# An encoder layer on one core: low weight tiles at another offset, two more first transposes, token block 0 finished first, and longer runs of high and low products in the up projection

## The chip, the core and the metric

The kernel runs on one of the eight cores of a Trainium2 chip. A core has a matmul engine (PE, with its weight loads shown as PEld), a vector engine (DVE), an activation engine (ACT), a general engine (POOL), a queue engine that issues most transfers (SP), and sixteen DMA engines between its on-chip memory and HBM. The metric is the device time of one execution in microseconds; the median of three runs is given.

## The reference

One layer of an encoder on 256 tokens of width 2048, and a final normalisation:

```
h = rms_norm(x);  proj = h @ w_in                    # 2048 x 9216
y_a = gated spatial MLP of (u, v)                    # 8 groups, chunks of 128 tokens
y_b = neighbourhood attention of (q, k, v)           # 16 heads on a 4 x 64 grid
merged = sigmoid(g_a) * (y_a @ Wb_a) + sigmoid(g_b) * (y_b @ Wb_b)
x = x + merged @ w_out
h = rms_norm(x);  up = h @ w_up                      # 2048 x 11008
up = depthwise conv of width 3 over tokens
x = x + (silu(gate) * val) @ w_down                  # 5504 x 2048
return rms_norm(x)
```

All inputs and outputs are float32, and the weights, some 64 million numbers, are read once.

## The kernel before, in words

**Products.** Each float32 operand is split in two: a high part, rounded by ACT to the matmul's own 32-bit format (`high`, L267), and a low part, the rest, which DVE subtracts (`low`, L270). A product is then three matmuls: high by high, low token part by high weight, and high token part by low weight.

**The stream of weights.** The weights are laid out in the order of use, in pieces of at most 128 x 1024 numbers (512 KB), and `weight_stream` names the order: the first group, the u and v columns, the attention's q, k and v with the gates between them, the branches, the output projection, and then twice an up projection over half of the 43 channel tiles and the down projection that follows it. For each piece i, `begin` issues loads as far as raw buffers are free (five), converts pieces up to i + 4 (`prepare`, as far as a pair of high and low buffers is free: four, and two more from the output projection on), and runs the tasks that earlier steps have put down for it (copies out of the banks, the convolution, and so on). Then the group's step writes the matmuls of piece i. Nothing else sets the order: each engine runs its instructions in the order in which the program was written, and waits on tiles. `unit_done` gives a pair of buffers back, and a later piece's conversion waits until the matmuls that read them are over.

**Weight-stationary groups.** The u columns, q and k, and the up projection (kind `ws`) hold the weights in the array and stream the tokens through. The token tile has the high parts of the 256 tokens and then their low parts, so one matmul of 512 columns on a high weight tile (L371) makes two of the three products, and one of 256 columns on a low weight tile (L377) the third. A piece has two row tiles by four column tiles of 128, so eight high products and eight low ones; a group has eight pieces and four banks. `spread_products` writes the high ones first in even pieces and the low ones first in odd pieces, so that across pieces they stand in runs of 16. Of the up projection there are 21 such groups, and one with two banks.

**The low tile's place.** A low tile is allocated with 64 numbers to spare (`LINE`), and in `ws` groups its data begin at `LOW_AT` numbers. All weight tiles and token tiles of the program begin 224 bytes past a multiple of 256; low data of `ws` groups therefore lie on a multiple of 256 before.

**The end.** The last group, the down projection's second half of columns, keeps its last four pieces back and finishes one bank after the other (`by_block`), each with 12 matmuls: the two token blocks t of 128 tokens by two column blocks of 512. As a bank is done, `finish` adds it to the residual on DVE, squares it on ACT with a sum, and multiplies by the final norm's weights (third quarter on POOL, fourth on DVE). `root` makes one over the root of the mean square for a token block, and `scaled` multiplies a stretch of columns by it on DVE or ACT and issues its store.

**The start.** `keep_awake` puts `WAKE` transposes of an identity ahead of the first product (L599), which start as soon as the identity is made.

Of the kernel before, what the change touches and what calls it, by code (L numbers as in the profile page):

```python
# [8 lines left out]
F32 = mybir.dt.float32  # L9
F32R = mybir.dt.float32r  # L10
AF = mybir.ActivationFunctionType
OP = mybir.AluOpType
AX = mybir.AxisListType
PSUM = bass.MemoryType.PSUM

T = 256
D = 2048
# [19 lines left out]
RMS_EPS = 1e-6  # L37
# [2 lines left out]
BLOCK = 1024  # L40
AHEAD = 5
RAW, UNITS, HALVES = 5, (4, 2), 1
WAKE = 18
EARLY = 4
SPLIT = 3
LINE = 64
LOW_AT = 8

FF_BLOCKS = ((0, 22), (22, 43))
FF_SEVEN = ((3, 5, 7), (2, 4, 6))  # L50
# [106 lines left out]
def trunk_kernel(ctx, tc, x, weights, vectors, ln_g, ln_b, w_s_turned, b_s, rpb, norm_final, out):  # L157
    nc = tc.nc
# [14 lines left out]
    const = keep("const")  # L173
    wpool = keep("weights")
    tmp = keep("tmp")
    hpool = keep("hT")
# [19 lines left out]
    pieces, _ = weight_pieces()  # L196
    kinds = {key: g[0] for key, g in weight_stream()[0].items()}
    size_of = {key: len(g[2]) for key, g in weight_stream()[0].items()}
    starts = {}
# [51 lines left out]
    def unit_done(key):  # L251
        slot = units.pop(key)[2]
        if slot[0] not in gone:
            unit_free.append(slot)
# [106 lines left out]
        prepare(i + AHEAD - 1)  # L361
        run_tasks(i)

    def spread_products(ps, n, last, i, acts, m):
        h, l, _ = units[i]
        tiles = len(pieces[i][2])

        def highs(k):
            for b, p in enumerate(ps):
                c = k * m + b * 128  # L370
                nc.tensor.matmul(p, h[:, c:c + 128], acts(2 * n + k), start=n == 0 and k == 0,  # L371
                                 stop=last and k == tiles - 1)

        def lows(k):
            for b, p in enumerate(ps):
                c = k * m + b * 128
                nc.tensor.matmul(p[:, :T], l[:, c:c + 128], acts(2 * n + k)[:, 0, :], start=False, stop=False)  # L377

        for f in (highs, lows) if n % 2 == 0 else (lows, highs):
            for k in range(tiles):  # L380
                f(k)

    def three_products(p, x, w, start, stop):
        xh, xl = x
# [47 lines left out]
    def ws_step(key, acts, done):  # L432
        box = {}

        def step(i):
            n, last = i - starts[key], i == starts[key] + size_of[key] - 1
            m = pieces[i][5]
            if n == 0:
                box["ps"] = [bank() for _ in range(m // 128)]
            spread_products(box["ps"], n, last, i, acts, m)  # L440
            unit_done(i)
            if last:
                done(box["ps"], i + 1)
        return step

    def wide_step(key, acts, sevens, rest, done, by_block=0, fresh=None):
# [70 lines left out]
        def step(i):  # L517
            n = i - n0
            c0, c1 = slice(0, 512), slice(512, 1024)
            if n in firsts:  # L520
                k = tiles[n]
                h, l, _ = halves[i]
                hb, lb, _ = units[i, "b"]
                product(1, acts(k, 0), (h, l))
                product(2, acts(k + 1, 0), (hb[:, c0], lb[:, c0]))
                product(3, sevens(k)[3], (hb[:, c1], lb[:, c1]))
                half_free.append(halves.pop(i)[2])
                unit_done((i, "b"))
            elif n - 1 in firsts:
                k = tiles[n - 1]  # L530
                ht, lt, _ = units[i - 1, "t"]
                hs, ls, _ = units[i - 1, "s"]
                S = sevens(k)
                product(5, S[0], (ht[:, c0], lt[:, c0]))
                product(7, S[2], (ht[:, c1], lt[:, c1]))
                unit_done((i - 1, "t"))
                product(6, S[1], (hs[:, c1], ls[:, c1]))
                product(4, acts(k + 1, 1), (hs[:, c0], ls[:, c0]))
                unit_done((i - 1, "s"))
                if n - 1 == firsts[-1]:  # L540
                    combine(i)
            elif n < size - by_block:
                h, l, _ = units[i]
                for (b, c), u in OUT.items():
                    cs = slice(c * 512, (c + 1) * 512)
                    product(u, acts(tiles[n], b), (h[:, cs], l[:, cs]))
                unit_done(i)
            elif n == size - 1:
                for b, c in ((0, 0), (1, 0), (0, 1), (1, 1)):
                    u = OUT[b, c]  # L550
                    for m in range(size - by_block, size):
                        h, l, _ = units[n0 + m]
                        cs = slice(c * 512, (c + 1) * 512)
                        product(u, acts(tiles[m], b), (h[:, cs], l[:, cs]))
                    done(p(u), b, c, i + 1)
                    free(p(u))
                for m in range(size - by_block, size):
                    unit_done(n0 + m)
            if n == size - 1 and not by_block:
                for (b, c), u in OUT.items():  # L560
                    done(p(u), b, c, i + 1)
                    free(p(u))
# [601 lines left out]
    def finish(p, t, q):  # L1164
        x2, ss = rs["x2"], fin["ss"]
        if q == 2:
            add_down(p, t, 2)
            v = x2[:, t, 1024:1536]
            nc.gpsimd.tensor_mul(v, v, fin["g", 2])
            part = fin["part", t] = const.tile([128, 1], F32, name=f"part{t}")  # L1170
            nc.vector.tensor_reduce(part, ss[:, t, 0:3], axis=AX.X, op=OP.add)
            nc.vector.tensor_scalar(part, part, 1.0 / D, RMS_EPS, op0=OP.mult, op1=OP.add)
            return
        v = x2[:, t, 1536:]
        nc.vector.tensor_add(v, p, v)
        nc.scalar.activation(junk, v, AF.Square, accum_out=ss[:, t, 3:4])
        fin["y", t] = hpool.tile([128, 512], F32, name=f"h{t}")
        if t == 0:
            nc.vector.tensor_mul(fin["y", 0], v, fin["g", 3])
            root(0)  # L1180
        else:
            scaled(0, 0, 512, nc.vector, nc.sync)
            scaled(0, 512, 1024, nc.vector, nc.sync)
            root(1, lambda: (nc.vector.tensor_mul(fin["y", 1], v, fin["g", 3]),
                             scaled(0, 1024, 1536, nc.scalar, nc.sync)))
            scaled(1, 640, 1536, nc.scalar, nc.scalar)
            scaled(1, 0, 640, nc.vector, nc.sync)
            scaled(1, 1536, 2048, nc.vector, nc.sync)
            scaled(0, 1536, 2048, nc.vector, nc.sync)

    def root(t, meanwhile=None):
        a, r, q, e, both = (const.tile([128, 1], F32, name=f"{n}3{t}") for n in "arqeb")
        nc.vector.tensor_scalar(a, fin["ss"][:, t, 3:4], 1.0 / D, fin["part", t], op0=OP.mult, op1=OP.add)
        nc.scalar.activation(q, a, AF.Sqrt)
        if meanwhile:
            meanwhile()
        nc.vector.reciprocal(r, q)
        nc.vector.scalar_tensor_tensor(e, r, r, a, op0=OP.mult, op1=OP.mult)
        nc.vector.tensor_scalar(e, e, -0.5, 1.5, op0=OP.mult, op1=OP.add)
        nc.vector.tensor_mul(both, r, e)  # L1200
        fin["r", t] = both
# [205 lines left out]
```

## Time and profile before

| what | value |
| --- | --- |
| median of three runs | 1315.31 us (1315.12 to 1316.0) |
| profiled execution, own time | 1315.79 us |
| its span, first to last instruction | 1313.6 us |
| granted matmul clock, mean | 0.998 |
| PE, PEld, DVE, ACT, POOL busy | 1302.2, 1109.9, 1015.1, 746.9, 99.5 us |
| high products in `ws` groups (L371) | 1760, 426.4 us busy |
| low products in `ws` groups (L377) | 1760, 228.5 us busy |
| up projection, two stretches | about 596 to 843 us and 959 to 1193 us |
| sum that follows the last matmul | starts at 1303.97 us |

How to read the rows: a group gives line, engine, operation, output tile, operands and shape, the count, busy microseconds and the mean nanoseconds of one, and idle time before it with what ended it. A row of the timeline gives start, length, engine, line, operation, tiles, shape and count. Matmuls are pipelined, so the length of one is longer than its share of the time; the distance from one start to the next is what it costs. A row of the chain of waits gives start, length, what ran, and how many in a row. A row of waits gives who waited for whom, the sum, how often, and the longest.

### The profile page before, as it was taken

The page shows a single profiled execution, that of the slowest core. Times are in us where ns is not written, and L with a number is a line of the kernel's source. Part 1 is how long each engine was busy: PE and PEld are TensorE (multiplying, and loading weights), DVE is VectorE, ACT ScalarE, POOL GpSimd, SP SyncE. Part 2 cuts the span into 40 slices and gives each one's busy share as a digit, 9 for nine tenths or more (in the row PEclk, how much of TensorE's full clock was granted, in tenths as well). Part 3 has the DMA queues.
Part 4 walks back from the last instruction along what each step waited for, and adds up shares of the span by engine and source line. Part 5 has one row for each costly group of instructions (what it writes and reads, how often), then busy time and mean ns, then how long its engine had stood idle before and what let it go on. Part 6 is the DMA issues. An engine that isn't in the chain of part 4 may idle for free.

```text
span 1313.6 us, 18614 instructions
## 1 busy us (share of the span) xinstructions
PE 1302.2 (99%) x6752; PEld 1109.9 (84%) x6752; DVE 1015.1 (77%) x1485; ACT 746.9 (57%) x1103; POOL 99.5 (8%) x192
## 2 busy tenths in 40 slices
PE   9999999999999999999999999999999999999997
PEld 8888888888888888888888888888888888888885
DVE  5577667767588978887878787898958787869987
ACT  5755567576545545555655555554535555546554
POOL 0502065430000000000000000000000000000000
PEclk9999999999999999999999999999999999999999
DMA  8957685655646566665655656557656656546653
GB/s 329 320 177 208 206 223 183 202 160 177 192 158 243 181 202 233 220 207 176 193 193 186 197 181 203 165 172 234 210 186 192 192 191 194 180 142 224 230 171 128
DMA packets 74044, 261.42 MB, mean 199 GB/s; under 512 B 9568, under 2 KB 10720, under 8 KB 73440
## 3 DMA queue, kind: packets, MB, share of 16 engines
q1 hardware_dynamic: 69984, 252.46, 59.3%
q0 software_dynamic: 3680, 7.30, 2.1%
q8 instruction: 53, 0.87, 0.3%
q10 hardware_dynamic: 288, 0.47, 0.1%
q14 instruction: 39, 0.32, 0.1%
HBM read 256.00 MB, written 2.10 MB: 196 GB/s over the span
## 4 chain that ended last, share of the span: by engine, by line
PE 92%; DMA 3%; DVE 3%; ACT 1%; issue 1%; POOL 0%; DVEq 0%; ACTq 0%; POOLq 0%
PE bank L371 29%; PE bank L377 15%; PE bank L386 15%; PE bank L388 15%; PE bank L387 15%; DMA wraw<-in_weights_dram 2%; DMA start<-in_weights_dram 1%; DVE wlo L270 1%; ACT whi L267 1%; PE bank L868 1%; PE bank L920 0%; PE bank L599 0%; PE bank L404 0%; PE bank L403 0%; DVE x L1034 0%
## 5 line engine op out<-in xcount | busy, mean ns | idle before, releaser
L270 DVE TENSOR_TENSOR wlo<-wraw,whi 128x1024 fp32r<-128x1024 f32 (+1 forms) x476 | 571.0, 1216 | 158.6 <-ACT whi L267 154.4
L267 ACT ACTIVATE whi<-wraw 128x1024 fp32r<-128x1024 f32 (+1 forms) x476 | 489.0, 1046 | 240.8 <-PE bank L387 76.3
L371 PE MATMUL bank<-h,whi 128*128 128x512 f32 x1760 | 426.4, 393 | 0.0
L371 PEld LDWEIGHTS bank<-h,whi 128*128 128x128 f32 x1760 | 321.6, 188 | 64.2
L377 PEld LDWEIGHTS bank<-h,wlo 128*128 128x128 f32 x1760 | 224.5, 188 | 10.3 <-DVE wlo L270 0.5
L377 PE MATMUL bank<-h,wlo 128*128 128x256 f32 x1760 | 228.5, 281 | 0.3 <-DVE wlo L270 0.3
L386 PE MATMUL bank<-whi,h 128*128 128x512 f32 x284 | 111.8, 394 | 0.0
L388 PE MATMUL bank<-wlo,h 128*128 128x512 f32 x284 | 110.7, 390 | 0.0
L387 PE MATMUL bank<-whi,h 128*128 128x512 f32 x284 | 110.6, 389 | 0.0
L388 PE MATMUL bank<-wlo,a 128*128 128x512 f32 x248 | 96.6, 389 | 0.0
L386 PE MATMUL bank<-whi,a 128*128 128x512 f32 x248 | 96.5, 389 | 0.0
L387 PE MATMUL bank<-whi,a 128*128 128x512 f32 x248 | 96.5, 389 | 0.0
L1097 ACT ACTIVATE tc<-ta,vec 128x256 f32<-128x256 f32 x86 | 47.1, 594 | 84.3 <-DVE ta L1095 84.3
L734 DVE TENSOR_TENSOR ta<-bank,tb 128x256 f32<-128x256 f32 x110 | 39.0, 417 | 67.2 <-ACT tb L732 67.2
L732 ACT ACTIVATE tb<-bank 128x256 f32<-128x256 f32 x110 | 36.2, 383 | 90.7 <-PE bank L371 85.1
L388 PEld LDWEIGHTS bank<-wlo,h 128*128 128x128 f32 x284 | 53.3, 188 | 11.3
L386 PEld LDWEIGHTS bank<-whi,h 128*128 128x128 f32 x284 | 53.3, 188 | 11.0
L387 PEld LDWEIGHTS bank<-whi,h 128*128 128x128 f32 x284 | 53.4, 188 | 10.7
L388 PEld LDWEIGHTS bank<-wlo,a 128*128 128x128 f32 x248 | 46.5, 188 | 10.0 <-DVE wlo L270 0.3
L387 PEld LDWEIGHTS bank<-whi,a 128*128 128x128 f32 x248 | 46.6, 188 | 9.7
L386 PEld LDWEIGHTS bank<-whi,a 128*128 128x128 f32 x248 | 46.5, 188 | 9.6
L1354 POOL DMA_DIRECT2D h<-in_norm_final_dram x4 | 2.2, 540 | 674.7 <-DVE wlo L270 674.2
(209 smaller groups left out, 1584.0 us busy)
## 6 DMA issues: line engine op xcount, KB each, us to landing
wraw<-in_weights_dram SPq DMA_DIRECT2D x446, 512.0 KB, 4.4
start<-in_weights_dram SPq DMA_DIRECT2D x13, 640.0 KB, 6.0
xs<-in_x_dram SPq DMA_DIRECT2D x2, 1024.0 KB, 10.1
vw<-va POOLq DMA_DIRECT2D x32, 64.0 KB, 5.9
x<-in_x_dram POOLq DMA_DIRECT2D x2, 1024.0 KB, 9.1
wraw<-in_weights_dram SPq DMA_DIRECT2D x8, 256.0 KB, 2.8
run<-in_rpb_dram POOLq DMA_DIRECT2D x64, 31.2 KB, 4.3
out_dram<-x SPq DMA_DIRECT2D x5, 256.0 KB, 2.9
```

The lines of the kernel that those rows point to most:

```text
L267: nc.scalar.activation(h, w, AF.Copy)
L270: nc.vector.tensor_sub(l, w, h.bitcast(F32))
L371: nc.tensor.matmul(p, h[:, c:c + 128], acts(2 * n + k), start=n == 0 and k == 0, stop=last and k == tiles - 1)
L377: nc.tensor.matmul(p[:, :T], l[:, c:c + 128], acts(2 * n + k)[:, 0, :], start=False, stop=False)
L386: nc.tensor.matmul(p, xh, wh, start=start, stop=False)
L387: nc.tensor.matmul(p, xl, wh, start=False, stop=False)
L388: nc.tensor.matmul(p, xh, wl, start=False, stop=stop)
L732: nc.scalar.activation(t, p[:, T:], AF.Copy)
L734: nc.vector.tensor_add(a, p[:, :T], t)
L868: nc.tensor.matmul(o, Q[s][:, c], k.rearrange("p (r c) -> p r c", r=ROWS)[:, :, k0:k0 + UNION], start=n == 0, stop=n == 1)
L1097: nc.scalar.activation(v, u, AF.Identity, scale=ck[:, 1, ch:ch + 1], bias=ck[:, 3, ch:ch + 1])
L1354: nc.gpsimd.dma_start(fin["g", j], bass.AP(tensor=norm_final.tensor, offset=norm_final.offset + j * 512, ap=[[0, 128], [1, 512]]))
```

## The change

Four edits:

1. `LOW_AT` goes from 8 to 56 numbers, so the low data of `ws` groups begin 224 bytes into their tile instead of 32.
2. `WAKE` goes from 18 to 20.
3. `spread_products` gets the group's first piece, its size and a flag. With the flag (the up projection alone) pieces are taken in fours: the highs of piece 0 and piece 1, the lows of 0, 1, 2 and 3, the highs of 2 and 3; so low products, and high ones across groups of four, stand in runs of 32. Buffers are given back in pairs, behind the odd piece. Without the flag the order is as before.
4. At the end, the banks are finished in the order (t 0, third quarter), (t 0, fourth), (t 1, third), (t 1, fourth), where the third quarters of both blocks came first. `finish` is written for it: block 0's root follows its fourth quarter, its first 1024 columns are scaled by ACT and stored at once, its third quarter by DVE behind block 1's third sum, and its fourth quarter behind block 1's fourth sum.

```diff
-WAKE = 18
+WAKE = 20
...
-LOW_AT = 8
+LOW_AT = 56
...
-    def spread_products(ps, n, last, i, acts, m):
-        h, l, _ = units[i]
-        tiles = len(pieces[i][2])
-
-        def highs(k):
...
-        for f in (highs, lows) if n % 2 == 0 else (lows, highs):
+    def spread_products(ps, first, n, size, acts, m, long):
+
+        last = size - 1
+
+        def highs(n):
+            h = units[first + n][0]
+            tiles = len(pieces[first + n][2])
             for k in range(tiles):
-                f(k)
+                for b, p in enumerate(ps):
+                    c = k * m + b * 128
+                    nc.tensor.matmul(p, h[:, c:c + 128], acts(2 * n + k), start=n == 0 and k == 0,
+                                     stop=n == last and k == tiles - 1)
+
+        def lows(n):
+            l = units[first + n][1]
+            for k in range(len(pieces[first + n][2])):
+                for b, p in enumerate(ps):
+                    c = k * m + b * 128
+                    nc.tensor.matmul(p[:, :T], l[:, c:c + 128], acts(2 * n + k)[:, 0, :], start=False, stop=False)
+
+        fours = (((highs, n),), ((highs, n), (lows, n - 1), (lows, n)), ((lows, n),),
+                 ((lows, n), (highs, n - 1), (highs, n)))
+        twos = ((highs, n), (lows, n)), ((lows, n), (highs, n))
+        for f, k in fours[n % 4] if long else twos[n % 2]:
+            f(k)
+        if not long:
+            unit_done(first + n)
+        elif n % 2:
+            unit_done(first + n - 1)
+            unit_done(first + n)
...
-            spread_products(box["ps"], n, last, i, acts, m)
-            unit_done(i)
+            spread_products(box["ps"], starts[key], n, size_of[key], acts, m, key[0] == "up")
...
-                for b, c in ((0, 0), (1, 0), (0, 1), (1, 1)):
-                    u = OUT[b, c]
+                for (b, c), u in OUT.items():
...
-            part = fin["part", t] = const.tile([128, 1], F32, name=f"part{t}")
-            nc.vector.tensor_reduce(part, ss[:, t, 0:3], axis=AX.X, op=OP.add)
-            nc.vector.tensor_scalar(part, part, 1.0 / D, RMS_EPS, op0=OP.mult, op1=OP.add)
+            if t == 0:
+                first_squares(0)
+            else:
+                scaled(0, 1024, 1536, nc.vector, nc.sync)
             return
...
-        fin["y", t] = hpool.tile([128, 512], F32, name=f"h{t}")
+        if t == 1:
+            first_squares(1)
+            scaled(0, 1536, 2048, nc.vector, nc.sync)
+        y = fin["y", t] = hpool.tile([128, 512], F32, name=f"h{t}")
+        nc.vector.tensor_mul(y, v, fin["g", 3])
+        root(t)
         if t == 0:
-            nc.vector.tensor_mul(fin["y", 0], v, fin["g", 3])
-            root(0)
+            scaled(0, 0, 1024, nc.scalar, nc.sync)
         else:
-            scaled(0, 0, 512, nc.vector, nc.sync)
-            scaled(0, 512, 1024, nc.vector, nc.sync)
-            root(1, lambda: (nc.vector.tensor_mul(fin["y", 1], v, fin["g", 3]),
-                             scaled(0, 1024, 1536, nc.scalar, nc.sync)))
             scaled(1, 640, 1536, nc.scalar, nc.scalar)
             scaled(1, 0, 640, nc.vector, nc.sync)
             scaled(1, 1536, 2048, nc.vector, nc.sync)
-            scaled(0, 1536, 2048, nc.vector, nc.sync)
```

`first_squares` is the pair of steps taken out of `finish` (the sum over three quarters, and the mean with its epsilon), and `root` loses the work that was put under its square root.

Inside an up group, at its fifth piece, the matmul engine changes from high products to low ones here (`whi` and `wlo` are weight tiles, `h` a token tile):

```order
L371 MATMUL bank3_6032<-h9_5825,whi4_6028 128x512
L371 MATMUL bank1_6033<-h9_5825,whi4_6028 128x512
L371 MATMUL bank2_6034<-h9_5825,whi4_6028 128x512
L371 MATMUL bank7_6035<-h9_5825,whi4_6028 128x512
L377 MATMUL bank3_6032<-h8_5824,wlo4_6029 128x256
L377 MATMUL bank1_6033<-h8_5824,wlo4_6029 128x256
L377 MATMUL bank2_6034<-h8_5824,wlo4_6029 128x256
L377 MATMUL bank7_6035<-h8_5824,wlo4_6029 128x256
```

and in the changed kernel at the same place (high products are written at its line 374, low ones at its line 382):

```order
L374 MATMUL bank3_6034<-h9_5827,whi4_6030 128x512
L374 MATMUL bank1_6035<-h9_5827,whi4_6030 128x512
L374 MATMUL bank2_6036<-h9_5827,whi4_6030 128x512
L374 MATMUL bank7_6037<-h9_5827,whi4_6030 128x512
L374 MATMUL bank3_6034<-h10_5837,whi5_6048 128x512
L374 MATMUL bank1_6035<-h10_5837,whi5_6048 128x512
L374 MATMUL bank2_6036<-h10_5837,whi5_6048 128x512
L374 MATMUL bank7_6037<-h10_5837,whi5_6048 128x512
```

The next piece's high products have come ahead of this piece's low ones.

Behind the last matmul, from the sum of the last bank on, DVE has before:

```order
L1175 TENSOR_TENSOR x2_5085<-bank4_12066,x2_5085 128x512
L1209 TENSOR_SCALAR x2_5085<-x2_5085,b30_12444 128x512 x2
L1193 TENSOR_SCALAR a31_12470<-ss_3_162,part1_12421 128x1
L1184 TENSOR_TENSOR h1_12465<-x2_5085,h5_11746 128x512
L1197 RECIPROCAL r31_12471<-q31_12472 128x1
L1198 SCALAR_TENSOR_TENSOR e31_12473<-r31_12471,a31_12470 128x1
L1199 TENSOR_SCALAR e31_12473<-e31_12473 128x1
L1200 TENSOR_TENSOR b31_12474<-r31_12471,e31_12473 128x1
L1209 TENSOR_SCALAR x2_5085<-x2_5085,b31_12474 128x640
L1209 TENSOR_SCALAR x2_5085<-h1_12465,b31_12474 128x512
L1209 TENSOR_SCALAR x2_5085<-h0_12438,b30_12444 128x512
```

and in the changed kernel (a, q, r, e and b are the steps of `root`, numbered 30 for block 0 and 31 for block 1):

```order
L1186 TENSOR_TENSOR x2_5087<-bank4_12068,x2_5087 128x512
L1203 TENSOR_REDUCE part1_12468<-ss_3_164 128x1
L1204 TENSOR_SCALAR part1_12468<-part1_12468 128x1
L1222 TENSOR_SCALAR x2_5087<-h0_12422,b30_12428 128x512
L1192 TENSOR_TENSOR h1_12473<-x2_5087,h5_11748 128x512
L1208 TENSOR_SCALAR a31_12475<-ss_3_164,part1_12468 128x1
L1210 RECIPROCAL r31_12476<-q31_12477 128x1
L1211 SCALAR_TENSOR_TENSOR e31_12478<-r31_12476,a31_12475 128x1
L1212 TENSOR_SCALAR e31_12478<-e31_12478 128x1
L1213 TENSOR_TENSOR b31_12479<-r31_12476,e31_12478 128x1
L1222 TENSOR_SCALAR x2_5087<-x2_5087,b31_12479 128x640
L1222 TENSOR_SCALAR x2_5087<-h1_12473,b31_12479 128x512
```

Two scalings of block 0 have left this place and one has moved up, the two small steps of `first_squares` have come in, and the multiplication into h1 now stands ahead of a31.

More of the change, by code (lines that the diff above doesn't have):

```diff
@@ L362, in begin @@
         run_tasks(i)
-    def spread_products(ps, n, last, i, acts, m):
-        h, l, _ = units[i]
-        tiles = len(pieces[i][2])
-        def highs(k):
[L369 to L377, printed above, removed]
-        for f in (highs, lows) if n % 2 == 0 else (lows, highs):
-            for k in range(tiles):
-                f(k)
+    def spread_products(ps, first, n, size, acts, m, long):
[3 more added lines that the diff above has]
+            tiles = len(pieces[first + n][2])
+            for k in range(tiles):
+                for b, p in enumerate(ps):
[18 more added lines that the diff above has]
+            unit_done(first + n)
     def three_products(p, x, w, start, stop):
@@ L1188, in finish, with first_squares, root @@
             scaled(1, 1536, 2048, nc.vector, nc.sync)
-            scaled(0, 1536, 2048, nc.vector, nc.sync)
-    def root(t, meanwhile=None):
+    def first_squares(t):
+        part = fin["part", t] = const.tile([128, 1], F32, name=f"part{t}")
+        nc.vector.tensor_reduce(part, fin["ss"][:, t, 0:3], axis=AX.X, op=OP.add)
+        nc.vector.tensor_scalar(part, part, 1.0 / D, RMS_EPS, op0=OP.mult, op1=OP.add)
+    def root(t):
         a, r, q, e, both = (const.tile([128, 1], F32, name=f"{n}3{t}") for n in "arqeb")
@@ L1194, in root @@
         nc.scalar.activation(q, a, AF.Sqrt)
-        if meanwhile:
-            meanwhile()
         nc.vector.reciprocal(r, q)
```

## The prediction

> **What bounds the kernel now.** First the page, to see which engine fills the span; then who waits for whom, to see whether that engine ever stands still; then the chain of waits and the timeline, for the pace of the products at the places which the change touches.
>
> ```profile
> PE 1302.2 (99%) x6752; PEld 1109.9 (84%) x6752; DVE 1015.1 (77%) x1485; ACT 746.9 (57%) x1103; POOL 99.5 (8%) x192
> PEclk9999999999999999999999999999999999999999
> ...
> L371 PE MATMUL bank<-h,whi 128*128 128x512 f32 x1760 | 426.4, 393 | 0.0
> ...
> L377 PE MATMUL bank<-h,wlo 128*128 128x256 f32 x1760 | 228.5, 281 | 0.3 <-DVE wlo L270 0.3
> ```
>
> Matmuls fill the span and the granted clock is full. The answer on waits has two rows for the matmul engine:
>
> ```profile
> PE bank L599 <- POOL ident masks.py:199: 1.4, 1, 1.4
> PE bank L377 <- DVE wlo L270: 0.3, 1, 0.3
> ```
>
> That is 1.7 us in all. So between the first product and the last the time is a count of products times their pace. Only three things can move the end: the pace of products, what stands ahead of the first one, and what follows the last one. The change touches all three. The pace is read from the chain of waits (start, length, what), over runs of 16, and at the last, narrower pair of blocks (1183 us on) over runs of 8:
>
> ```profile
> 628.20 1.89 PE bank L377 x16
> 630.09 3.68 PE bank L371 x16
> ...
> 1183.18 0.94 PE bank L377 x8
> 1184.13 1.86 PE bank L371 x8
> 1185.99 0.95 PE bank L377 x8
> 1186.93 1.83 PE bank L371 x8
> ```
>
> Low products (L377) cost 1.89/16 = 118 ns each, high ones (L371) 3.68/16 = 230 ns. Is 230 what a 512-column product must cost? The timeline of matmuls shows a stretch without a low product of half width, by its first and its 57th matmul, and then one run of 16 high products cut at its tenth:
>
> ```profile
> 1195.31 0.39 PE L386 MATMUL bank<-whi,a 128*128 128x512 f32 x1
> ...
> 1208.00 0.39 PE L388 MATMUL bank<-wlo,s 128*128 128x512 f32 x1
> ```
>
> ```profile
> 629.93 2.25 PE L371 MATMUL bank<-h,whi 128*128 128x512 f32 x9
> ...
> 632.24 1.53 PE L371 MATMUL bank<-h,whi 128*128 128x512 f32 x6
> 633.61 0.28 PE L377 MATMUL bank<-h,wlo 128*128 128x256 f32 x1
> ```
>
> Undisturbed, the pace is (1208.00 - 1195.31)/56 = 226.6 ns. In the run, the first ten take 632.24 - 629.93 = 2.31 us (231 each), and the last six 633.61 - 632.24 = 1.37 us (228 each). So a run of high products that follows low ones loses 3.68 - 16 x 0.2266 = 0.055 us, nearly all of it in its first ten products. This is a price for each change from low to high, and the runs of four change half as often.
>
> **The runs of four, in the up projection.** The number of products, their operands and their banks stay; so do all instructions of the other engines up to the last block, in the same order. A group of eight pieces has four low runs of 16 now and two of 32 after. There are 21 such groups and one of half width, so 22 x 2 = 44 changes from low to high go. If a longer low run leaves the same disturbance behind, this saves 44 x 0.055 = 2.4 us. The other bound comes from the runs of 8: their two high runs lose 1.86 + 1.83 - 16 x 0.2266 = 0.064 us for 16 low products, against 0.055 us for one run of 16, so doubling the length there saved only 0.009. If doubling it again saves a like share (14% of 0.110 per 32 products), that is 0.015 x 44 = 0.7 us. I take 2.3, near the upper end: a high run is at its undisturbed pace again after ten products, so how far behind the low run put it is bounded, and low products themselves cost 118 ns in runs of 8 as in runs of 16 (0.945/8 against 1.89/16), so they do not become slower as the run goes on.
>
> The Trainium skill (TensorE: Matmul & The Clock Gate, Back-to-back issue gap) speaks against this term: it gives a gap of N / 2.4 + 2.5 ns for a warm isolated matmul, which is 216 ns for 512 columns and 109 for 256, with no term for what ran before. By it the reordering would save nothing. The trace doesn't bear the figures out (227 and 118).
>
> A pair of pieces is now given back together, so a high tile's buffer is freed up to one piece later. A piece takes (1.89 + 3.68)/2 = 2.79 us; conversions run four pieces, some 11 us, ahead of their use, and cost about 1.05 on ACT and 1.22 on DVE. Six buffers are just enough for two held pieces and four ahead. Queued behind a later conversion on ACT are the copies that empty the banks; they wait for matmuls anyway:
>
> ```profile
> ACT whi L267 <- PE bank L371: 46.7, 31, 2.7
> ACT tb L732 <- PE bank L371: 85.1, 25, 4.2
> ```
>
> One piece later leaves 8 us of cover: cost 0. If the cover were gone, each of 88 pairs could cost up to a piece.
>
> **Low tiles at 224 bytes.** Only the place changes from which low weights are read (and written). Writing it costs nothing: the subtraction takes the same time at the present 32 bytes and at none, as the groups of two windows show, the up projection and the down projection behind it.
>
> ```profile
> L270 DVE TENSOR_TENSOR wlo<-wraw,whi 128x1024 fp32r<-128x1024 f32 x85 | 102.8, 1220 | 14.3 <-ACT whi L267 14.3
> ...
> L270 DVE TENSOR_TENSOR wlo<-wraw,whi 128x1024 fp32r<-128x1024 f32 x50 | 59.9, 1220 | 9.7 <-ACT whi L267 9.3
> ```
>
> For reading it no row has two places. Bounds: half of an undisturbed 512-column product is 113.3 ns, so a low product carries an excess of 118.2 - 113.3 = 4.9 ns. At best it vanishes, 1760 x 4.9 = 8.6 us, and with it what is left of the losses after low runs (1760/16 = 110 runs less 44, 3.6 us): -12.2. At worst I let it double (an estimate): +8.6. The middle of these is -1.8; the nearest row is the present placement, also 32 bytes from its neighbours' alignment but on the other side (tiles lie 224 bytes past a multiple of 256), and says 0. Between the two I take -0.7, which is 0.4 ns per low product.
>
> The Trainium skill (SBUF — State Buffer, two separate sides) says that TensorE's reads never wait on another engine, and gives no cost to an address; by it this term is 0, and the sum 0.7 us higher. No run here shows one or the other.
>
> **Two more transposes ahead.**
>
> ```profile
> 1.38 4.10 PE L599 MATMUL bank<-ident 128*128 128x128 f32 x18 [1.38 <-POOL ident masks.py:199]
> ...
> 5.13 0.77 PE L403 MATMUL bank<-whi,h 128*128 128x512 f32 x1
> 5.70 0.63 PE L404 MATMUL bank<-whi,h 128*128 128x512 f32 x1
> 6.13 0.63 PE L403 MATMUL bank<-whi,h 128*128 128x512 f32 x1
> ...
> 7.53 0.39 PE L403 MATMUL bank<-whi,h 128*128 128x512 f32 x1
> 7.76 0.39 PE L404 MATMUL bank<-whi,h 128*128 128x512 f32 x1
> ```
>
> Eighteen start within 5.13 - 1.38 = 3.75 us, 0.21 each, so two add 0.43. The second product waits 0.57 after the first where the next follow at 0.43, so 0.14 is absorbed; 0.29 of slow time remains, which is two thirds of a product, worth 0.15 at the fast pace. Bounds: 0 (the wait of 0.3 on the low tile takes it up) and 0.43. I take 0.1.
>
> **The tail.** Last matmul to end: the sum on DVE starts at 1303.97, the span ends at 1313.6.
>
> ```profile
> 1303.97 0.68 DVE L1175 TENSOR_TENSOR x<-bank,x 128x512 f32<-128x512 f32 x1
> 1304.57 0.87 DVE L1209 TENSOR_SCALAR x<-x,b 128x512 f32<-128x512 f32 x2
> 1304.74 0.63 ACT L1176 ACTIVATE junk<-x 128x512 f32<-128x512 f32 x1 [1.53 <-DVE x L1175]
> 1305.07 3.88 SPq L1210 DMA_DIRECT2D out_dram<-x  x6
> 1305.50 0.21 DVE L1193 TENSOR_SCALAR a<-ss,part 128x1 f32<-128x1 f32 x1
> 1305.63 0.68 DVE L1184 TENSOR_TENSOR h<-x,h 128x512 f32<-128x512 f32 x1
> 1306.87 0.16 DVE L1200 TENSOR_TENSOR b<-r,e 128x1 f32<-128x1 f32 x1
> 1307.06 0.55 DVE L1209 TENSOR_SCALAR x<-x,b 128x640 f32<-128x640 f32 x1
> 1307.53 0.88 DVE L1209 TENSOR_SCALAR x<-h,b 128x512 f32<-128x512 f32 x2
> 1308.19 0.34 ACTq L1210 DMA_DIRECT2D out_dram<-x  x1
> ```
>
> Now DVE runs two scalings of token block 0 while ACT squares, and h is multiplied under the root. After, DVE has behind the sum at 1304.57: two small steps (0.35), one scaling (0.44) and the multiplication (0.68 to 0.85), and only then a, at 1306.1 to 1306.3 instead of 1305.50. From a to the end of b takes 1.3 to 1.5 now (h stands in between), 1.3 after. So b is 0.4 to 0.6 later; but one scaling fewer stands behind it (0.44), so compute ends about where it did. The gain is in the output queue: of 2 MB, issued from 1305.07 on, 1280 KB follow behind 1307.5 now and 1024 KB after, since block 0's sum can start 24 matmuls (5.4 us) before block 1's and 768 KB of it leave by about 1304. As 2 MB take at most the 8.5 us from 1305.07 to the span's end, 256 KB take at most 1.1, and some 0.9 if the last 1.2 us are the program's end. Bounds -0.9 and +0.5 (POOL's product, 1.3 us long, now meets DVE's work there); I take -0.3.
>
> **Sum.** -2.3 - 0.7 + 0.1 - 0.3 = -3.2 us. The profiled execution took 1315.8 around its span of 1313.6; the median of the runs is 1315.3, so 1312.1.
>
> **Rivals.** (B) The place of the low tiles matters much: low products near 115 ns. For it: the excess of 4.9 ns stands only in low products, which alone are read from another alignment. Against: nothing in the trace varies the place. 1760 x 3.2 = 5.6 us beside the 2.5 of the rest: 1307. (C) The runs of four save nothing, because a run twice as long leaves twice the disturbance; the runs of 8 speak for that in part, the recovery within ten products against. Then -0.9 and 0 to -0.3 remain: 1314.6, which is no change. (D) The other side: the new place slows the low products. It decides from 118.2 + (2.6 + 2.5)/1.76 = 121.1 ns on; at 122 the cost is 1760 x 3.8 = 6.7 against 2.5 saved: 1319.5. For it: its price stands on all 1760 low products, 384 of which get no longer runs.
>
> **Chances.** Forecast 0.48 (its own range 1309.5 to 1314), B 0.22, C 0.20, D 0.10. A measurement of this kernel can tell about 0.2%, 2.6 us, from no change. Faster than that: all of B and two thirds of the forecast, 0.55; slower: most of D, 0.08; the rest, 0.37, is within. The range takes in B's time and stops short of D's: 1306 to 1316.
>
> **What would show it.** In the changed profile the up projection's chain should read 3.78 for 32 low products and 7.30 to 7.31 for 32 high ones. High runs of 7.36 mean C. Low runs of 16 in the earlier stages, whose order stays, give the place alone: 1.88 by the forecast, 1.84 for B, 1.95 for D. A row of PE waiting for the low or high tiles would mean that held buffers bite. The first product should start near 5.56, and the end lie 9.4 us behind the last sum. The forecast is wrong if the low pace moves by over 1.5 ns.

## The result, and the profile after

| | before | after |
| --- | --- | --- |
| median of six runs each | 1315.49 us (1315.12 to 1316.0) | 1310.78 us (1310.51 to 1311.18) |
| ratio, 95% interval | | 0.9964 (0.9953 to 0.9976) |
| profiled execution: own time, span | 1315.79, 1313.6 us | 1310.80, 1308.7 us |
| start of the last matmul | 1303.52 us | 1297.06 us |
| from there to the end of the span | 10.12 us | 11.66 us |

The change is 4.7 us faster. Inside that stand two numbers of opposite sign: the products became 6.5 us shorter, and the end became 1.5 us longer.

The page of the changed kernel, the rows that answer to those shown of before:

```profile
PE 1296.1 (99%) x6754; PEld 1107.3 (85%) x6754; DVE 1015.0 (78%) x1484; ACT 746.4 (57%) x1103; POOL 100.6 (8%) x192
PEclk9999999999999999999999999999999999999998
...
L374 PE MATMUL bank<-h,whi 128*128 128x512 f32 x1760 | 415.8, 391 | 0.0
L382 PE MATMUL bank<-h,wlo 128*128 128x256 f32 x1760 | 218.7, 280 | 0.0
```

The matmul engine still fills the span at full clock, and it waits for nothing but the identity ahead of its first transpose. So what moved is the pace of products and the end. The pace is read from the chain of waits (start, length, what), first in an early stage whose order of products did not change, then in the up projection:

```profile
63.20 1.87 PE bank L382 x16
65.07 3.66 PE bank L374 x16
...
1102.28 3.73 PE bank L382 x32
1106.02 7.29 PE bank L374 x32
```

Before, 16 low products took 1.89 us everywhere and 16 high ones 3.68. The early pair is 1.87 + 3.66 now: that is the place of the low tile alone, 0.04 us for each of 24 such pairs, 1 us. In the up projection four pieces take 3.73 + 7.29 = 11.02 us, where two pairs of before took 2 x (1.89 + 3.68) = 11.14: 0.12 to 0.13 us for each of some 43 cycles, 5.4 us. Together 6.4 of the 6.5.

Then the end, from the timeline of the changed kernel, from the last sum on:

```profile
1297.49 0.69 DVE L1186 TENSOR_TENSOR x<-bank,x 128x512 f32<-128x512 f32 x1
1297.59 5.43 SPq L1223 DMA_DIRECT2D out_dram<-x  x5
1298.25 1.26 POOL L1179 TENSOR_TENSOR x<-x,h 128x512 f32<-128x512 f32 x1 [3.62 <-ACT junk L1158]
1298.47 1.33 DVE L1222 TENSOR_SCALAR x<-h,b 128x512 f32<-128x512 f32 x1
1300.32 0.20 DVE L1208 TENSOR_SCALAR a<-ss,part 128x1 f32<-128x1 f32 x1
1302.10 0.48 DVE L1222 TENSOR_SCALAR x<-h,b 128x512 f32<-128x512 f32 x1
```

Two scalings of the same size stand in it: the one at 1302.10 takes 0.48 us, the one at 1298.47 takes 1.33. The longer one overlaps POOL's product (1298.25 to 1299.51) and ends 0.29 us behind it. So a starts 1300.32 - 1297.49 = 2.83 us behind the start of the sum; before, it was 1305.50 - 1303.97 = 1.53.

That alone does not set the end, as the view of the program's last line shows. Its row for POOL's own queue gives the shortest, median and longest drain in ns, and the first and last start; of the changed kernel:

```profile
L1415 POOLq DRAIN  x3: 46/98/9719, 1298.2 to 1308.5; - x3
```

and of the kernel before:

```profile
L1402 POOLq DRAIN  x3: 46/98/9752, 1300.9 to 1313.4; - x3
```

The stores of the kernel before, by the output tensor they write, with their first and last start and the times from issue to landing:

```profile
L1210 SPq DMA_DIRECT2D out_dram<-x x6: 332/360/424, 1305.1 to 1308.5; - x6
...
DMA to landing us min/median/max: 2.3/2.9/4.2
```

and those of the changed kernel:

```profile
L1223 ACTq DMA_DIRECT2D out_dram<-x x1: 350/350/350, 1302.8 to 1302.8; - x1
...
DMA to landing us min/median/max: 2.6/2.8/3.6
```

Behind its last product POOL's queue has a drain instruction. The long drain starts with that product at 1298.2 and ends 9.72 us later, at 1307.9, which is 8.42 us after the product's own end. In the changed kernel the last store lands at 1306.3 (issued at 1302.8, 3.6 earlier), so the span waits 1.6 us longer for the drain, and closes 0.8 behind it. Before, the drain was over at 1310.7 while the last store, issued at 1308.5, landed at 1312.7: it was covered. POOL's last product of before shows why, in the timeline of that engine:

```profile
1300.96 1.30 POOL L1169 TENSOR_TENSOR x<-x,h 128x512 f32<-128x512 f32 x1 [0.44 <-ACT junk L1148]
```

It was over 1.3 us ahead of the start of the last matmul; in the new order of banks it is over 2.45 us behind that start (1299.51 against 1297.06). The stores alone would cost next to nothing: the last one lands 9.27 us behind the start of the last matmul, against 9.20 before.

The start shows no loss in this pair of traces. The timeline of the changed kernel:

```profile
1.38 4.53 PE L609 MATMUL bank<-ident 128*128 128x128 f32 x20 [1.38 <-POOL ident masks.py:199]
5.56 0.78 PE L415 MATMUL bank<-whi,h 128*128 128x512 f32 x1
6.13 0.60 PE L416 MATMUL bank<-whi,h 128*128 128x512 f32 x1
6.56 0.41 PE L415 MATMUL bank<-whi,h 128*128 128x512 f32 x1
6.80 0.40 PE L416 MATMUL bank<-whi,h 128*128 128x512 f32 x1
```

The first product starts 0.43 us later, as forecast, but only two products run at the slow pace where before four or five did, and the 64th product starts at 20.44 in one and at 20.46 in the other.

### The profile page after: what moved, and what is told of

It reads as the page before. It is cut to its first block, busy times and chain, and to the rows that moved or that the text cites. A ratio compares the mean times of both kernels' runs of the same rounds, so it can differ in the third digit from the quotient of the medians.

```text
span 1308.7 us, 18617 instructions
## 1 busy us (share of the span) xinstructions
PE 1296.1 (99%) x6754; PEld 1107.3 (85%) x6754; DVE 1015.0 (78%) x1484; ACT 746.4 (57%) x1103; POOL 100.6 (8%) x192
## 4 chain that ended last, share of the span: by engine, by line
PE 96%; DVE 1%; DMA 1%; ACT 1%; issue 0%; POOL 0%; ACTq 0%; POOLq 0%; DVEq 0%
PE bank L374 31%; PE bank L382 16%; PE bank L398 15%; PE bank L400 15%; PE bank L399 15%; PE bank L415 1%; PE bank L416 1%; PE bank L418 1%; DMA wraw<-in_weights_dram 1%; PE bank L878 1%; DVE wlo L270 0%; PE bank L930 0%; PE bank L609 0%; DVE x L1044 0%; PE bank L752 0%
## 5 line engine op out<-in xcount | busy, mean ns | idle before, releaser
L374 PE MATMUL bank<-h,whi 128*128 128x512 f32 x1760 | 415.8, 391 | 0.0
L382 PEld LDWEIGHTS bank<-h,wlo 128*128 128x128 f32 x1760 | 215.9, 188 | 6.1
L382 PE MATMUL bank<-h,wlo 128*128 128x256 f32 x1760 | 218.7, 280 | 0.0
```

## Experiments

The theory after this comparison: (1) each change from low to high products costs a bounded 0.055 us at the old place, so that runs of four save 2.4; (2) the byte at which a low tile begins sets the pace of its products, worth some 4 us; (3) the end lost 1 to 1.5 us, to POOL's product. The rivals: the gain is all place, or all order; and the end's loss is something else, such as a late start of the stores.

### One part of the change at a time

runs_only is the kernel before with the new `spread_products` and its call alone; place_only has `LOW_AT` alone; end_only the new order of banks and the new `finish` alone; old_end is the changed kernel with those two put back.

```diff
 runs_only   +            spread_products(box["ps"], starts[key], n, size_of[key], acts, m, key[0] == "up")
 place_only  -LOW_AT = 8
             +LOW_AT = 56
 end_only    -                for b, c in ((0, 0), (1, 0), (0, 1), (1, 1)):
             +                for (b, c), u in OUT.items():
             (and finish, first_squares, root as in the change)
 old_end     the reverse of end_only, made to the changed kernel
```

> The kernel before with runs of four in the up projection, and nothing else. Theory one (a high run loses 0.055 us after any low run, whatever its length; the place adds to that independently): 44 losses fewer, 2.4 us, so 1313.1 beside 1315.5; 32 low products take 3.78 us and 32 high ones 7.31. Rival (the loss grows with the low run, and the gain seen in the changed kernel is the place's alone): 32 high products take 7.36, no gain, 1315.5.

> The kernel before with low tiles at 224 bytes, and nothing else. In the changed kernel, the early stages, whose runs of 16 stay, have low runs of 1.864 us (1.892 before) and high runs of 3.662 (3.673 there, 3.682 in the up projection before). Theory one: these hold in the up projection too, so 110 times 0.028 + 0.02 = 5 us: 1310.5. Rival (the place does most of its work only together with long runs): about 1313.5, a gain near 2.

> The kernel before with the changed end (token block 0 first), and nothing else. Theory one (POOL's product of block 1 now lies in the last 4 us: it holds up DVE's scaling for 0.9 us, and the program's end waits for POOL to drain, 8.4 us behind that product): the end is 1.5 us further behind the last matmul, so 1317.0. Rival (the changed end costs what its chain on DVE costs, and the drain is not waited for): at most 0.6 longer, 1316.0. As predicted at first: 0.3 us shorter, 1315.2.

> The changed kernel with the end of the kernel before (third quarters first, old order of finish). Theory one: 1.5 us less than the changed kernel, 1309.3, with the last matmul to the end in 10.1 us. If the changed end is worth the 0.3 us first predicted: 1311.1.

| run | median | ratio to before, 95% interval | last matmul starts | from there to the end |
| --- | --- | --- | --- | --- |
| runs_only | 1312.96 | 0.9981 (0.9972 to 0.999) | 1300.8 | 10.16 |
| place_only | 1311.08 | 0.9963 (0.995 to 0.9975) | 1298.8 | 10.15 |
| end_only | 1316.28 | 1.0008 (1.0 to 1.0017) | 1303.3 | 11.15 |
| old_end | 1309.25 | 0.9952 (0.994 to 0.9965) | 1296.7 | 10.44 |

The order of products is worth 2.4 us, the place 4.3, and the end costs 0.9, each against 1315.4 for before in the same session; in the changed kernel the end costs 1.5 (1310.78 against old_end's 1309.25, from two sessions). The three single parts sum to -5.8, the whole is -4.7. Medians with intervals of 1 us and more on either side do not show an overlap by themselves; the traces do, below. Chains of waits show the two parts that touch the products; runs_only:

```profile
623.51 3.79 PE bank L382 x32
627.30 7.31 PE bank L374 x32
```

and place_only:

```profile
627.23 1.87 PE bank L377 x16
629.10 3.66 PE bank L371 x16
```

The rows of the chain are rounded; by start times (from the first product of a run to the first product behind it), four pieces took 11.15 us before. With the old place and the new order they take 11.09, and low products keep their 118 ns; with the new place and the old order 11.05; with both 11.02. So each part has a trace of its own, and neither "all place" nor "all order" stands. The parts overlap: the new order saves 0.054 us a cycle at the old place and 0.034 at the new one, where the first high products behind a low run lose less. Over the two stretches of the up projection runs_only saves 2.25 us, place_only 3.97 and the changed kernel 5.41.

The end by itself (end_only): its stores land earlier relative to the products than before, not later. The last matmul starts at 1303.34 and the last store lands at 1312.13, 8.79 us on, against 1312.72 - 1303.52 = 9.20 before. But the drain's row reads

```profile
L1404 POOLq DRAIN  x3: 46/98/9719, 1304.0 to 1314.2; - x3
```

so it is over at 1304.0 + 9.72 = 1313.7, behind the stores, and the span ends at 1314.5, again 0.8 behind it. The median of 1316.28 lies between the two expectations, nearer to the rival's 1316.0, and its interval reaches down to no change; it is the drain row that speaks for the theory. The end is 1.0 longer here and not 1.5 because POOL's product is over 1.94 us behind the start of the last matmul, and not 2.45 as in the changed kernel.

### Does a longer low run leave more behind it?

lengths is the changed kernel with runs of one, two and four pieces in turn by groups, low tiles at 32 bytes in the first half of the up projection and at 224 in the second.

```diff
+def low_at(key):
+    return 8 if key[0] == "up" and key[1] < 22 else LOW_AT
+def run_of(key):
+    return (1, 2, 4)[key[1] // 2 % 3] if key[0] == "up" else 2
```

> The changed kernel, with the runs of the up projection's groups in turn of one, two and four pieces, and the low tiles at 32 bytes in its first half and at 224 in its second. Theory one (a loss per change, of 0.055 us at 32 bytes and about 0.035 at 224, whatever the length): at 32 bytes a group of eight pieces costs 22.29 us in runs of two and 22.18 in runs of four, and about 22.4 in runs of one; at 224 bytes 22.10, 22.04 and 22.2. Rival (the loss grows with the run): groups of the three kinds cost the same to 0.05 us at each place.

It took 1313.87 us. From its chain of waits, first half (L390 low, L382 high):

```profile
732.71 0.94 PE bank L390 x8
733.65 1.86 PE bank L382 x8
...
749.45 1.89 PE bank L390 x16
751.34 3.68 PE bank L382 x16
...
779.13 3.79 PE bank L390 x32
782.91 7.31 PE bank L382 x32
```

32 high products at the undisturbed 226.6 ns would take 7.25. Behind 32 lows a high run loses 0.06 us, behind 16 lows 3.68 - 3.626 = 0.055, behind 8 lows about half of that (0.064 for the two runs of 8 that the prediction shows). At 32 bytes the loss saturates at 16: halving the changes halves it. At 224 bytes it is 0.035 to 0.037 by start times, behind 8, 16 and 32 lows alike. The low products' own pace at 32 bytes is 118 ns at each length. Four pieces in runs of one, two and four take 11.16, 11.15 and 11.09 us at 32 bytes by start times, and 11.12, 11.05 and 11.02 at 224.

### Which place, and how fine does it matter?

places puts each up group's low tiles at 0, 32, 64 ... 224 bytes in turn; places_fine at 88, 96, 104, 208, 216, 232, 240 and 248 bytes (with the end of new_end, below).

```diff
+PLACES = (0, 8, 16, 24, 32, 40, 48, 56)
+def low_at(key):
+    return PLACES[key[1] // 2 % 8] if key[0] == "up" else LOW_AT
```

> The changed kernel, with the low tiles of the up projection's 22 groups in turn at 0, 32, 64, 96, 128, 160, 192 and 224 bytes. Read from each group's runs of 32. Theory one (what matters is the distance of the low reads from the other tiles' alignment, in steps, with some places good and some bad): at 32 bytes 3.78 us for 32 low products, at 224 3.73, and others between 3.63 (no excess) and 3.94 (double), a spread of over 0.1 us. Rival (the place matters little, and 32 and 224 happen to differ by 0.05): all within 3.72 to 3.79.

> new_end with the low tiles of the up projection's groups in turn at 88, 96, 104, 208, 216, 232, 240 and 248 bytes. At 96 bytes 32 low and 32 high products cost 3.757 + 7.265 = 11.02 us, at 224 bytes 3.732 + 7.284 = 11.02. Theory one (the cost goes by whole steps of 32 bytes): 208 and 216 read as 192 (11.07) and 232 to 248 as 224. Rival (by smaller steps): places between 11.0 and 11.1 with no such steps, one of them perhaps lower than 11.0.

The medians say little here (1312.83 and 1309.27); the rows are the result. Time of 32 low products by the byte at which their tile's data begin:

| byte | 0 | 32 | 64 | 88 | 96 | 104 | 128 | 160 | 192 | 208 | 216 | 224 | 232 | 240 | 248 |
| --- | --- | --- | --- | --- | --- | --- | --- | --- | --- | --- | --- | --- | --- | --- | --- |
| us | 3.83 | 3.78 | 3.77 | 3.65 | 3.76 | 3.77 | 3.84 | 3.84 | 3.77 | 3.73 | 3.82 | 3.73 | 3.79 | 3.75 | 3.77 |

The chain of waits of places, for the slowest place, 128 bytes:

```profile
689.12 3.84 PE bank L387 x32
```

and of places_fine, for 88, 96 and 216 bytes:

```profile
612.25 3.65 PE bank L387 x32
615.90 7.28 PE bank L379 x32
623.18 3.76 PE bank L387 x32
626.94 7.26 PE bank L379 x32
...
689.33 3.82 PE bank L387 x32
693.14 7.30 PE bank L379 x32
```

Each place comes back with the same length in the next groups that have it. The spread is 3.65 to 3.84, 114 to 120 ns per product, and 8 bytes (88 against 96) move it by 0.11. Neither the distance to a multiple of 32, of 64 nor of 256 orders the row; what does is left open, and so is the way in which the place acts, since it is where DVE writes the low tile as well as where the matmul engine reads it. The old place (3.78) was not a bad one, the new one is good, and 88 is better by another 0.08, with high products of the same length as at 224 (7.28).

at_88 then has all low tiles of `ws` groups at 88 bytes, with the end of new_end.

```diff
-LOW_AT = 56
+LOW_AT = 22
```

> The changed kernel with the old order of copy and drain at the end already rearranged as in the run new_end, and the low weight tiles at 88 bytes of their 256-byte cells, not 224; nothing is left out. Theory one (the byte offset of a low tile sets the pace of its product): 32 low products take 3.65 us instead of 3.73 in all 44 cycles of the up projection, about 3.9 us, and about 1 us more in the early stages: 1303 us, ratio to the kernel before about 0.991. The rival (the 88 bytes of the fine scan were good only where groups of other offsets stood beside them, or the gain is taken back by the high products): 1308 us, as new_end.

It took 1303.91 us, ratio 0.991 (0.9893 to 0.9926): 4 us under new_end, and 11.9 under the kernel before. Its chain of waits:

```profile
623.09 3.65 PE bank L382 x32
626.74 7.28 PE bank L374 x32
```

and its row of low products among the groups by line:

```profile
L382 PE MATMUL bank<-h,wlo 128*128 128x256 f32 x1760 | 214.6, 278 | 0.6 <-DVE wlo L270 0.6
```

3.65 for 32 in every cycle, as where the groups were mixed: the pace belongs to the place. (11.02 - 10.93) x 43 = 3.9 us of it stand in the up projection. The matmul engine now waits 0.6 us once for a low tile; the changed kernel had no such wait.

### What the end waits for

late_on_dve is the changed kernel with POOL's last product (block 1's third quarter) moved to DVE, behind the scaling. new_end moves it under block 1's square root and joins block 1's last multiplication and scaling into one instruction. late_pool is the kernel before with one copy of 128 x 1 numbers on POOL that waits for the last b.

```diff
 late_on_dve  -            nc.gpsimd.tensor_mul(v, v, fin["g", 2])          (t = 1)
              +            nc.vector.tensor_mul(x2[:, 1, 1024:1536], x2[:, 1, 1024:1536], fin["g", 2])
 new_end      +            root(1, lambda: nc.vector.tensor_mul(x2[:, 1, 1024:1536], x2[:, 1, 1024:1536], fin["g", 2]))
              +            nc.vector.scalar_tensor_tensor(v, v, fin["r", 1], fin["g", 3], op0=OP.mult, op1=OP.mult)
 late_pool    +            nc.gpsimd.tensor_copy(const.tile([128, 1], F32, name="late"), fin["r", 1])
```

> The changed kernel with block 1's product of the third quarter on DVE (behind the scaling of block 0's last quarter) and not on POOL. Theory one (the program's end waits for POOL's drain, 8.4 us behind its last product): compute ends about where it does now (POOL's lock on DVE, 0.9 us, goes, and a product of 0.7 comes), but POOL has drained long before, and the end follows the last store by 0.9 us: 1.3 less than the changed kernel, 1309.5. Rival (the 2.4 us between the last store's landing and the end are something else): no change, 1310.8.

> As late_on_dve, but with that product under block 1's square root, and block 1's last quarter multiplied by its weights and by the root in one DVE instruction. Theory one: b 0.7 to 1.0 us earlier than in the changed kernel, stores that land by 1305.5, the end 2.2 us less than the changed kernel: 1308.6. Rival (the end is bound elsewhere): 1309.5 or more.

> The kernel before with one tiny POOL instruction added, a copy of block 1's root (one number per partition), 3.5 us behind the last matmul's start; nothing reads the copy. Theory one (POOL's drain at the program's end lasts some 9.7 us from its last instruction, whatever that is): the drain ends near 1317, 4 us behind where the stores let the program end now, and the time rises by 4: 1319.4. Rival (the drain's length belongs to the 512-column product, or the end doesn't wait for it): no change, 1315.4.

| run | median | ratio to before, 95% interval | last matmul to the end | drain over | last store landed |
| --- | --- | --- | --- | --- | --- |
| late_on_dve | 1308.76 | 0.995 (0.9936 to 0.9964) | 9.86 | 1304.1 | 1307.0 |
| new_end | 1307.97 | 0.9943 (0.9929 to 0.9956) | 9.60 | 1303.5 | 1305.9 |
| late_pool | 1325.75 | 1.0084 (1.0067 to 1.0101) | 12.95 | 1322.7 | 1319.7 |

With POOL's product gone from the end, 1.8 us (11.66 to 9.86) come back, and new_end wins another 0.3. In the timeline of new_end the same scaling takes 0.48 again, with DVE's own product behind it:

```profile
1298.92 0.48 DVE L1226 TENSOR_SCALAR x<-h,b 128x512 f32<-128x512 f32 x1
1299.41 0.21 DVE L1210 TENSOR_SCALAR a<-ss,part 128x1 f32<-128x1 f32 x1
1299.54 0.68 DVE L1197 TENSOR_TENSOR x<-x,h 128x512 f32<-128x512 f32 x1
```

a starts 1.67 us behind the sum of 1297.74, against 2.83. The Trainium skill (SBUF — State Buffer, two separate sides) says that one port pair is shared by VectorE and GpSimd as an exclusive lock, held for a whole instruction, and that a vector operation which needs it blocks behind a GpSimd operation. The trace agrees: the scaling that took 1.33 us ended 0.29 behind POOL's product, and took 0.48 without it. In end_only, where it started later under the product, it took 0.94 and again ended 0.29 behind it.

late_pool tests the drain alone. Its copy in the timeline:

```profile
1314.06 0.18 POOL L1186 COPY late<-b 128x1 f32<-128x1 f32 x1 [5.23 <-DVE b L1201]
```

and its drain, in the view of that line:

```profile
L1403 POOLq DRAIN  x3: 51/93/8624, 1314.0 to 1323.2; - x3
```

The drain starts with the waiting copy at 1314.0 and lasts 8.62: it is over 8.42 us behind the end of a 0.18 us copy, as it was 8.42 behind products of 1.3 us. So between these two it does not depend on the work, and the span (to 1323.5) waits for it. The end is 2.8 us longer by it.

### An unplanned seven microseconds

late_pool was expected at 1319.4 and took 1325.75. Only 2.8 us of the 10 are at the end; its last matmul starts at 1310.50, 7.0 us late. The theory: the added tile of 128 x 1 numbers had pushed all weight and token tiles 32 bytes up, from 224 past a multiple of 256 to a multiple of 256. all_moved does only that to the kernel before, with no added work:

```diff
-    const.tile([128, 56], F32, name="line")
+    const.tile([128, 64], F32, name="line")
```

> The kernel before with nothing changed but one small line tile made 32 bytes longer, so that all weight and token tiles behind it lie 32 bytes higher (224 to 0 modulo 256); no work is added. Theory one (the place of all stationary and moving tiles is what cost the run late_pool its 7 us in the products): about 1322.4 us, the last product 7 us later and the rest behind it unchanged at 10.1 us. The rival (the copy that was added on the POOL engine in late_pool cost the products their 7 us): 1315.4 us, as before.

It took 1323.16, ratio 1.0058 (1.0043 to 1.0073); its last matmul starts 7.0 us later than before and the rest is 10.13. So the place of all tiles costs these 7 us, and POOL's copy none of them. Its chain of waits in the up projection:

```profile
626.67 3.68 PE bank L371 x16
630.36 1.89 PE bank L377 x16
632.25 3.71 PE bank L371 x16
635.96 1.91 PE bank L377 x16
637.87 3.72 PE bank L371 x16
```

and from its timeline two matmuls, 57 apart, of the stretch in which the prediction read the undisturbed pace:

```profile
1199.24 0.39 PE L386 MATMUL bank<-whi,a 128*128 128x512 f32 x1
...
1212.37 0.39 PE L386 MATMUL bank<-whi,s 128*128 128x512 f32 x1
```

High runs vary between 3.68 and 3.72 now, and the stretch without half-width products goes at (1212.37 - 1199.24)/57 = 230.4 ns instead of 226.6. So the 226.6 that the prediction took for the undisturbed pace is itself a matter of place.

## Why the prediction was right, and where it was not

The forecast of 1312.1 us lies 1.3 above the 1310.78 measured, and its direction holds. But of the four terms one was right, one was not told apart, and two were off by more than the total is, in opposite directions. That the total came so near is in part luck.

**Runs of four, -2.3: right at the old place.** runs_only measured -2.4, and 7.31 for 32 high products is the number that was named. On top of the new place the order is worth 1.4 (5.41 - 3.97 in the up projection): the forecast added the two terms as if they were independent. The reason given, that a high run is back at its pace within ten products and so the loss is bounded, is what lengths shows. The lower bound, -0.7, was taken from runs of 8, which are too short to reach the full loss. Rival C (nothing saved, 7.36 per run) is out; by its own terms its time was 1314.1 to 1314.4, not 1314.6. The formula that the prediction took from the Trainium skill (TensorE: Matmul & The Clock Gate, Back-to-back issue gap) is given there for an isolated matmul, and it does not describe this stream: runs_only differs from before in the order of products, and the giving back of buffers that follows it, and is faster.

**Low tiles at 224 bytes, -0.7: mis-sized.** It is -4.3 alone, and about -4.1 with runs of four (0.07 us in each of 43 cycles, 11.09 against 11.02 in lengths, and 1 in the early stages). The bounds, -12.2 and +8.6, held it. The choice between them was the step that failed here: the nearest row, the present place, was read as "nothing", when it could not say whether the present place was a good or a bad one. Low products went to 3.73/32 = 116.6 ns, where the forecast had 117.8 and rival B 115: the truth lies halfway to B. The forecast named a move of 1.5 ns as what would make it wrong; it moved by 1.6. The Trainium skill (SBUF — State Buffer, two separate sides) states that TensorE's reads wait on no other engine and gives no price to an address, by which this term would be 0. place_only shows a price on the address, in whatever way it comes about.

**Two more transposes, +0.1: not told apart.** In the compared pair it is 0. But full pace does not come at one time: among the six traces here with 18 transposes the 64th product starts between 19.46 and 20.46, among the eight with 20 between 19.68 and 20.70. The means differ by 0.5, less than the spread of 1.0 within either set, so a cost of some tenths is neither shown nor excluded. No run changed this number alone.

**The end, -0.3: wrong sign, +1.5 (+0.9 alone).** The reasoning on stores was sound: with end_only and late_on_dve the last store lands 0.4 us sooner behind the last matmul. Two things took it back. POOL's product meeting DVE's work was in the range, as +0.5, priced as an overlap; it held a scaling until the product was over, 0.85 us, and so the stores of the changed kernel gained nothing (9.27 against 9.20). And the program's end was put down as "the last 1.2 us" behind the stores, without asking which engine it waits for: POOL's drain stood in the trace of before, ending 2 us ahead of the last store's landing, and the forecast has no term for it. The new order moved POOL's last product, and the drain with it, from 1.3 us ahead of the last matmul's start to 2.45 behind it: that was the cost missed, and it alone sets the +1.5. The end was to lie 9.4 us behind the start of the last sum; it lay 11.2 behind.

**Held buffers, 0: right.** No row of the matmul engine waiting for high or low tiles appeared; the one of 0.3 us before is gone.

**Rival D (the place slows, 1319.5)** did not happen at 224 bytes, but its mechanism exists: at 128 or 160 bytes low products take 3.84, 0.06 more than at the old place, and all_moved lost 7 us to a place. Had the sum been made with the measured -2.4, -4.1 (the place on top of the long runs), 0 and +1.5, it would have been -5.0, against the 4.9 by which the span shrank.

## What to carry to other kernels

Where the matmul engine fills the span, the byte at which its weight and token tiles begin is a size to be tuned: scan it in steps of 8 bytes with several places in one kernel and read the chain of waits by place, then check that later edits (one small tile in the same pool is enough) do not move it. Keep the end of the general engine's last instruction more than 9 us (8.42 and 0.8 here) away from the end, and off the moments in which the vector engine has the critical path. When an end is rearranged, list what every engine's queue is doing behind the last instruction, not only the stores.

## What the runs showed of the hardware that was not expected

- 256-column low products take 114.0 to 120.1 ns by the byte at which their weights begin, and 8 bytes can be worth 3.4 ns. 512-column products went from 226.6 to 230.4 ns when all tiles moved by 32 bytes.
- With low tiles at 32 bytes, the high products that follow a run of 16 or 32 low ones lose 0.055 to 0.06 us in all, and about half after 8; at 224 bytes they lose 0.035 to 0.037 after 8, 16 or 32.
- POOL's drain is over 8.42 us behind the end of its last instruction, whether that took 0.18 or 1.3 us, and the program's end waits for it; where the drain is the last to be over, the span closes 0.8 us behind it.
- A scaling of 128 x 512 on DVE takes 0.48 us alone and 1.33 when it starts 0.22 us into a POOL product of 1.26.
- The best version run here is at_88: 1303.91 us, ratio to the kernel before 0.991 (0.9893 to 0.9926).
